# Half token tile of a dense expert layer: one float32r operand of 128 columns in place of plain float32 on column halves

## Chip, cores and metric

The kernel runs on one core of a Trainium2 chip. The metric is device time in microseconds, the median of several executions of the whole program. A profile is one execution more.

## What is computed

Two layers of a diffusion backbone over 512 latent tokens and 256 context tokens of width 1024. Each layer has a token mixer and then PEER, a retrieval over 16384 single-neuron experts. The change lies in PEER:

```python
def peer(h, wq, keys, u_tab, v_tab):
    ...
    eid = jnp.take_along_axis(cid, top_p, axis=-1)
    gate = jax.nn.softmax(top_s, axis=-1).astype(xb.dtype)
    act = jax.nn.gelu(jnp.einsum('td,thkd->thk', xb, u_tab[eid]))
    return jnp.einsum('thk,thkd->td', gate * act, v_tab[eid])
```

Every token picks 16 of the experts for each of 8 heads, 128 in all. The result is a float32 sum over them.

## The kernel before

PEER treats part of the tokens densely and part by gathers. For the dense part the scores of all 16384 experts are computed, multiplied by a weight that is zero where an expert wasn't picked, and the product with the whole table V is formed on PE (TensorE). For the gathered part rows of the tables are fetched one expert slot at a time by indirect transfers from POOL (line 1123). In layer 0 384 tokens are dense, in layer 1 320: two full tiles of 128 tokens and a half tile of 64. The other 64 slots' worth of that tile and the last tile of 128 are gathered: 192 steps over the rows of U (`gtile_u`, line 1134 on DVE) and 192 over V (`gtile_v`, line 1147 on DVE).

The dense part is `peer_x`. The experts stand in 128 blocks of 128. `ublock(i)` loads 512 KB of U (transposed) into a buffer `uv`, splits it into a float32r part `uvh` (a copy on ACT, line 113) and a residue `uvl` (a subtraction on DVE, line 114), multiplies both with the split tokens (line 121, three passes: hi x lo, lo x hi, hi x hi) and writes the GeLU of the scores to slot i of a ring `PA`/`PB`. `weights(c, i)` multiplies the weights of 8 tokens and some 44 blocks into the ring; it takes small DVE operations, eight or so on ACT, and short float16 matmuls `pwt` (line 1267). `vblock(i)` loads 512 KB of V into `uv`, splits it in the same way, splits the slot's 256 columns of the two full tiles into `wh` and `wl`, and adds twelve float32r matmuls of 512 columns to the accumulators `dacc` in PSUM, two tiles by two halves of the row by three passes. The half tile is done apart (line 1290): two plain float32 matmuls whose operands are the 64 columns of the slot and the raw block, one for each half of the row; they write to partitions 0 to 63 and 64 to 127 of one bank.

There are two buffers of `uvh`, `uvl`, `wh` and `wl`, and in layer 1 three of `uv`. A loop over m runs from -nB to 127: first weights that are due, then `vblock(m)`, then `ublock(m + R)` with R = nA + nB, the slots of the ring (32 + 46 in layer 1). So after a fill of u blocks come 50 steps with a v and a u block, some 35 v blocks with weights, and the rest of the v blocks alone. At the end the accumulators are multiplied by a gain (lines 1332 and 1335), added to the residual and normalized (`ended`, lines 1172 to 1181).

A scheduler sets the order of the instructions on every engine when the program is built, by priorities (`prio`): the dense part of layer 1 has 5, its gathers 6, so a gather step is put where the scheduler sees room. Each engine then runs its list in order. Loads of `uv` are issued by SP, each as soon as its buffer is free and those ahead of it are issued.

Of the kernel before, what the change touches and what calls it, by code (L numbers as in the profile page):

```python
# [9 lines left out]
F32 = mybir.dt.float32  # L10
F32R = mybir.dt.float32r
# [4 lines left out]
ALU = mybir.AluOpType  # L16
# [4 lines left out]
D = 1024  # L21
# [24 lines left out]
ALL, LO, HI = slice(0, 128), slice(0, 64), slice(64, 128)  # L46
# [25 lines left out]
class Kern:  # L72
# [101 lines left out]
    def schedule(self):  # L174
        a = self.a
        with ExitStack() as er:
            ec = ExitStack()
            self.context(ec, 0)
            with self.banks("ctx0", "right", w=2, S=1) as ps, ExitStack() as e0:
                md = e0.enter_context(self.pool("mod", side="right"))  # L180
                pm = e0.enter_context(self.banks("mod", "right", w=1))
                fl = e0.enter_context(self.pool("flt"))
                pf = e0.enter_context(self.banks("flt", "left", w=2, S=1))
                with self.prio(1), ExitStack() as e:
                    self.filters(fl, pf, 0, LC)
                    self.modulation(md, pm, 0, 0, 2)
                    st = self.front(e, ps, ps, 0, 1, 1, side="right")
                    self.filters(fl, pf, 0, LX)
                    self.modulation(md, pm, 0, 2, 6)
                    self.back(ps, ps, 0, 1, st, None)  # L190
                    self.filters(fl, pf, 1, LX)
                    self.modulation(md, pm, 1, 0, 2)
            self.gp = er.enter_context(self.pool("gath", side="right"))
            with self.prio(1), self.banks("rc", "right", w=2) as ps:
                gc = self.route(ps, 0, 1, "GG", side="right")
            with self.banks("x0", "left", w=2, S=2) as ps:
                with ExitStack() as e:
                    with self.prio(3):
                        pr = e.enter_context(self.banks("x0b", "right", w=2))
                        st = self.front(e, ps, pr, 0, 0, 3, split=False)  # L200
                        ex, keep = ExitStack(), ExitStack()
                        rn = self.back(ps, pr, 0, 0, st, ex, keep=keep)
                        ex = (keep, ex)
                ec.close()
            with self.prio(6):
                self.gtile_u(0, gc[0])
                self.gtile_v(0, 1, 0, gc[0])
                self.gtile_u(0, gc[1])
            with self.prio(3):
                gx, ex = self.peer_x(0, 384, 6, 31, 33, (36, 46, 46), ex, rn)  # L210
            with self.prio(6):
                self.gtile_u(0, gx[3])
                self.gtile_v(0, 0, 3, gx[3])
                self.gtile_v(0, 1, 1, gc[1])
            with ExitStack() as ec, ExitStack() as e:
                self.context(ec, 1)
                ps = e.enter_context(self.banks("x1", "left", w=2, S=2))
                pr = e.enter_context(self.banks("x1b", "right", w=2))
                with self.prio(3):
                    st = self.front(e, ps, pr, 1, 0, 4, ctx=True)  # L220
                with self.prio(4):
                    self.back(ps, pr, 1, 0, st, None, (2, 6))
            with self.prio(5):
                gx, _ = self.peer_x(1, 320, 0, 32, 46, (44, 42, 42), (ex,))
            with self.prio(6):
                for i in sorted(gx, reverse=True):
                    self.gtile_u(1, gx[i])
                    self.gtile_v(1, 0, i, gx[i])
# [955 lines left out]
    def peer_x(self, l, T, vn, nA, nB, widths, done, rn=None):  # L1184
# [4 lines left out]
        nc, a = self.nc, self.a  # L1189
        nd, half = divmod(T, 128)  # L1190
        nt = nd + bool(half)
# [4 lines left out]
        with ExitStack() as es:  # L1196
# [7 lines left out]
            free = P[0].rearrange("p i t -> p (i t)")  # L1204

            def slot(i):
                i %= nA + nB
                return P[0][:, i, :] if i < nA else P[1][:, i - nA, :]
# [62 lines left out]
                                                   1.0 / GSCALE, dst, op0=ALU.mult, op1=ALU.mult)  # L1271

            def vblock(i, sp):
                r0 = l * NEXP + i * 128
                if vn and i % vn == vn - 1:
                    raw = dn.tile([128, D], F32, name="uv", bufs=2 + l)
                    nc.sync.dma_start(raw, a["peer_v"][r0:r0 + 128, :])
                    v, w = [raw], [slot(i)]
                else:
                    raw, v = block("v", a["peer_v"][r0:r0 + 128, :])  # L1280
                    w = [sp.tile([128, nd * 128], F32R, name=n, bufs=2) for n in ("wh", "wl")]
                    self.split(*w, slot(i)[:, :nd * 128])
                vh = [[x[:, h * 512:(h + 1) * 512] for x in v] for h in range(2)]
                for t in range(nd):
                    for h in range(2):
                        self.mm([acc[t][:, h * 512:(h + 1) * 512]], [[x[:, t * 128:(t + 1) * 128] for x in w]],
                                [vh[h]], i == 0, i == 127)
                if half:
                    for h in range(2):
                        nc.tensor.matmul(acc[nd][h * 64:(h + 1) * 64], slot(i)[:, nd * 128:T],  # L1290
                                         raw[:, h * 512:(h + 1) * 512], start=(i == 0), stop=(i == 127))

            fill = (ublock(i) for i in range(nA))
            with self.banks(f"r{l}", "right", w=2, S=2) as ps:
# [5 lines left out]
            sp = ew.enter_context(self.pool(f"dw{l}"))  # L1300
            if nB:
                P.append(sp.tile([128, nB, T], F32, name="PB"))
            pa = es.enter_context(self.banks(f"da{l}", "left", w=nt - nd, S=nd))
            acc = [pa.S(f"dacc{i}") if i < nd else pa.w(f"dacc{i}") for i in range(nt)]
            due = {}
            for c, w in enumerate(widths):
                m0, m1 = cuts[c + 1] - R, cuts[c]
# [10 lines left out]
            ex = None  # L1318
            if l == 0:
                ex = ExitStack()  # L1320
                self.res[0] = ex.enter_context(self.pool("xs1", side="right")).tile([128, 4, D], F32, name="xs")
            g2, fg, *rest = (free[:, i * D:(i + 1) * D] for i in range(2 + 2 * nt))
            nc.sync.dma_start(g2, bcast_rows(self.rows[l, 3, 0, :]))
            if l:
                nc.sync.dma_start(fg, bcast_rows(a["final_g"]))
# [3 lines left out]
            for t in range(nt):  # L1329
                res, y = rest[t], rest[nt + t]  # L1330
                if t < nd:
                    nc.vector.tensor_mul(y, acc[t], g2)
                else:
                    for h in range(2):
                        nc.vector.tensor_mul(y[LO, h * 512:(h + 1) * 512], acc[t][h * 64:(h + 1) * 64],
                                             g2[h * 64:(h + 1) * 64, h * 512:(h + 1) * 512])
                self.ended(dn, l, 0, t, ALL if t < nd else LO, y, res, res if l else self.res[0][:, t, :], fg)
        return gx, ex

# [126 lines left out]
```

## Time and profile before

| | us |
|---|---|
| median of 3 runs | 4270.21 (4254.28 to 4272.61) |
| the profiled execution | 4259.61 |
| its span on the core | 4257.7 |
| PE busy | 3709.5 (87%) |
| DVE (VectorE) busy | 3508.1 (82%) |
| ACT (ScalarE) busy | 1902.7 (45%) |
| POOL busy | 1524.0 (36%) |

PE is TensorE, PEld its loads of weights, SPq the queue on which SP issues transfers. Every time is counted from the start of the span. [...]

### The profile page before, as it was taken

Reading aid. Unit: us, or ns where it says so; the run is one execution under the profiler, and the core shown is the slowest. Engines: PE = TensorE matmul, PEld = TensorE weight load, DVE = VectorE, ACT = ScalarE, POOL = GpSimd, SP = SyncE. Lnnn points to the kernel's source line nnn. Section 1 sums busy time; section 2 is a strip of 40 time slices with the busy share of each in tenths; the row PEclk is TensorE's granted clock in tenths of the full one; section 3 lists DMA queues with packets and bytes.
Section 4 is the critical chain, followed back from the end, with each engine's and each line's share of the span. In section 5 each row is a group of like instructions: output and inputs, shape, how many; then the busy total and the mean of one; then the engine's idle time right before and its main releaser. Section 6 shows DMA issues by size and latency. Waiting matters only on the chain.

```text
span 4257.7 us, 63783 instructions
## 1 busy us (share of the span) xinstructions
PE 3709.5 (87%) x22514; PEld 2804.8 (66%) x22514; DVE 3508.1 (82%) x7449; ACT 1902.7 (45%) x3719; POOL 1524.0 (36%) x1225
## 2 busy tenths in 40 slices
PE   6887988967989999988968979888888999999997
PEld 3645544557878878877756656447888877776654
DVE  5746988889899989988898875754898988898988
ACT  4555243523247426622552244633334755555732
POOL 0000345642344564366436620000126345553243
PEclk7998998979989999999989989998999999999999
DMA  6655687885768897799879952242359888888697
GB/s 204 203 178 183 214 307 244 300 288 185 250 226 266 307 363 268 243 361 348 292 233 332 348 181 87 84 142 100 138 180 352 270 296 296 294 299 277 227 352 274
DMA packets 305634, 1063.74 MB, mean 250 GB/s; under 512 B 35756, under 2 KB 42624, under 8 KB 305314
## 3 DMA queue, kind: packets, MB, share of 16 engines
q0 software_dynamic: 165888, 604.05, 40.8%
q1 hardware_dynamic: 139426, 455.61, 30.7%
q8 instruction: 177, 2.90, 0.3%
q14 instruction: 143, 1.17, 0.1%
HBM read 1042.69 MB, written 16.84 MB: 249 GB/s over the span
## 4 chain that ended last, share of the span: by engine, by line
PE 32%; DMA 21%; DVE 19%; issue 16%; POOL 6%; ACT 5%; SPq 0%; POOLq 0%; DVEq 0%; ACTq 0%
PE pst L121 7%; POOL grow L1123 6%; PE dacc L121 6%; DMA grow<-in_peer_u_dram,eid 6%; DMA grow<-in_peer_v_dram,eid 5%; DMA uv<-in_peer_v_dram 4%; PE pwin L121 4%; DMA uv<-in_peer_ut_dram 3%; DVE uvl L114 3%; DVE acc L1147 3%; DVE acc L1134 2%; PE ppq L121 2%; DMA wmod<-in_w_mod_dram 2%; PE pwo L121 1%; PE fp L414 1%
## 5 line engine op out<-in xcount | busy, mean ns | idle before, releaser
L1123 POOL DMA_INDIRECT grow<-in_peer_u_dram,eid x576 | 749.6, 1301 | 1166.6 <-DVE acc L1134 591.8
L1123 POOL DMA_INDIRECT grow<-in_peer_v_dram,eid x576 | 766.8, 1331 | 748.0 <-DVE acc L1147 604.4
L121 PE MATMUL pst<-dhT,uvh 128*128 128x384 f32 (+1 forms) x4096 | 998.6, 328 | 0.0
L113 ACT CAST uvh<-uv 128x1024 fp32r<-128x1024 f32 x491 | 512.9, 1045 | 699.7 <-DMA uv<-in_peer_v_dram 422.4
L121 PE MATMUL pst<-dhT,uvl 128*128 128x384 f32 (+1 forms) x2048 | 695.2, 339 | 115.5 <-DVE uvl L114 83.9
L1147 DVE SCALAR_TENSOR_TENSOR acc<-grow,gate,acc 128x1024 f32<-128x1024 f32 x571 | 732.9, 1283 | 49.9 <-DMA grow<-in_peer_v_dram,eid 42.9
L1134 DVE SCALAR_TENSOR_TENSOR acc<-grow,ghx 128x1024 f32<-128x1024 f32 x576 | 704.4, 1223 | 73.4 <-DMA grow<-in_peer_u_dram,eid 68.4
L121 PEld LDWEIGHTS pst<-dhT,uvh 128*128 128x128 f32 x4096 | 730.6, 192 | 2.8 <-issue 1.2
L114 DVE TENSOR_TENSOR uvl<-uv,uvh 128x1024 fp32r<-128x1024 f32 x491 | 599.5, 1222 | 154.8 <-ACT uvh L113 152.1
L121 PEld LDWEIGHTS pst<-dhT,uvl 128*128 128x128 f32 x2048 | 394.2, 192 | 218.2 <-DVE uvl L114 163.5
L121 PE MATMUL dacc<-uvh,wl 128*128 128x512 f32 x1154 | 482.0, 418 | 40.1 <-ACT uvh L113 21.3
L121 PE MATMUL dacc<-uvl,wh 128*128 128x512 f32 x1154 | 468.8, 406 | 25.7 <-DVE uvl L114 25.4
L121 PE MATMUL dacc<-uvh,wh 128*128 128x512 f32 x1154 | 462.9, 401 | 0.0
L1263 ACT ACTIVATE o<-iota,di2n 128x128 f16<-128x128 f16 x1056 | 325.2, 389 | 27.6 <-PE pwt L1267 27.4
L121 PEld LDWEIGHTS dacc<-uvh,wl 128*128 128x128 f32 x1154 | 220.6, 191 | 130.3 <-ACT uvh L113 37.0
L121 PEld LDWEIGHTS dacc<-uvl,wh 128*128 128x128 f32 x1154 | 221.1, 192 | 84.5 <-DVE uvl L114 40.2
L121 PEld LDWEIGHTS dacc<-uvh,wh 128*128 128x128 f32 x1154 | 221.2, 192 | 47.9
L1267 PEld LDWEIGHTS <-o 128*128 128x128 f16 x4224 | 126.4, 97 | 104.3 <-issue 31.1
L1233 ACT ACTIVATE PA<-pst 128x320 f32<-128x320 f32 (+1 forms) x126 | 58.4, 463 | 290.4 <-PE pst L121 290.3
L1267 PE MATMUL pwt<-og,o 128*128 128x46 f16 (+3 forms) x4224 | 152.3, 183 | 37.1 <-DVE og L1253 29.7
L1233 ACT ACTIVATE PB<-pst 128x384 f32<-128x384 f32 (+1 forms) x130 | 60.0, 462 | 218.2 <-PE pst L121 218.1
L256 POOL MEMSET rmod<- 128x512 f32 (+1 forms) x8 | 3.3, 416 | 421.1 <-PE ptmod L282 171.8
(403 smaller groups left out, 6104.5 us busy)
## 6 DMA issues: line engine op xcount, KB each, us to landing
uv<-in_peer_ut_dram SPq DMA_DIRECT2D x256, 512.0 KB
uv<-in_peer_v_dram SPq DMA_DIRECT2D x256, 512.0 KB
wmod<-in_w_mod_dram SPq DMA_DIRECT2D x96, 512.0 KB
wpq<-in_peer_wq_dram SPq DMA_DIRECT2D x48, 512.0 KB
w_in<-in_w_in_dram SPq DMA_DIRECT2D x72, 256.0 KB
w_in<-in_w_in_dram SPq DMA_DIRECT2D x18, 512.0 KB
grow<-in_peer_u_dram,eid POOLq DMA_INDIRECT x576, 6.6
grow<-in_peer_v_dram,eid POOLq DMA_INDIRECT x576, 6.8
```

The lines of the kernel that those rows point to most:

```text
L113: self.nc.scalar.copy(hi, src)
L114: self.nc.vector.tensor_tensor(lo, src, hi.bitcast(F32), op=ALU.subtract)
L121: self.nc.tensor.matmul(p, w[i], x[j], start=start and n == 0, stop=stop and n == len(passes) - 1)
L256: nc.gpsimd.memset(r, 0.0)
L414: self.nc.tensor.matmul(p, w, x, start=(i == 0), stop=(i == len(pairs) - 1))
L1123: self.nc.gpsimd.indirect_dma_start(out=r, out_offset=None, in_=self.a[table], in_offset=bass.IndirectOffsetOnAxis(ap=eid[:, j:j + 1], axi ...
L1134: nc.vector.scalar_tensor_tensor(junk, r, 1.0, hx, op0=ALU.mult, op1=ALU.mult, accum_out=dot[:, j:j + 1])
L1147: nc.vector.scalar_tensor_tensor(acc, r, w[:, j:j + 1], acc, op0=ALU.mult, op1=ALU.add)
L1233: nc.scalar.activation(slot(i), p, AF.Gelu_apprx_tanh)
L1263: nc.scalar.activation(o2[:, q], self.iota, AF.Abs, bias=i2n[:, t, k * NC + q:k * NC + q + 1])
L1267: nc.tensor.matmul(p[:, q, :], o2[:, q, :], og[:, g, q, :], start=(g == 0), stop=(g == 1))
```

## The change

In layer 1 the copy on ACT now takes all 320 columns of the slot into one tile `both`, and DVE writes the residue of the half tile's 64 columns right behind their copies and the residue of the 256 columns at the end. The 128 columns in the middle (64 copies, 64 residues) are one operand. It is multiplied with `uvl` and with `uvh` for each half of the row: four float32r matmuls, into a third accumulator of two banks that holds the sums of the copies on partitions 0 to 63 and those of the residues on 64 to 127. At the end both are multiplied by the gain and added. `nB` of layer 1 goes from 46 to 45. Layer 0, without a half tile, gets the tile `both` too, with the same copy and the same single subtraction.

```diff
--- before.py
+++ after.py
@@ -221,7 +221,7 @@
                 with self.prio(4):
                     self.back(ps, pr, 1, 0, st, None, (2, 6))
             with self.prio(5):
-                gx, _ = self.peer_x(1, 320, 0, 32, 46, (44, 42, 42), (ex,))
+                gx, _ = self.peer_x(1, 320, 0, 32, 45, (44, 42, 42), (ex,))
             with self.prio(6):
                 for i in sorted(gx, reverse=True):
                     self.gtile_u(1, gx[i])
@@ -1271,15 +1271,23 @@
                                                    1.0 / GSCALE, dst, op0=ALU.mult, op1=ALU.mult)
 
             def vblock(i, sp):
                 r0 = l * NEXP + i * 128
+                F = nd * 128
                 if vn and i % vn == vn - 1:
                     raw = dn.tile([128, D], F32, name="uv", bufs=2 + l)
                     nc.sync.dma_start(raw, a["peer_v"][r0:r0 + 128, :])
                     v, w = [raw], [slot(i)]
                 else:
                     raw, v = block("v", a["peer_v"][r0:r0 + 128, :])
-                    w = [sp.tile([128, nd * 128], F32R, name=n, bufs=2) for n in ("wh", "wl")]
-                    self.split(*w, slot(i)[:, :nd * 128])
+                    both = sp.tile([128, 2 * T], F32R, name="w", bufs=2)
+                    w = [both[:, :F], both[:, 2 * T - F:]]
+                    nc.scalar.copy(both[:, :T], slot(i))
+                    for o, n, to in ((F, T - F, T), (0, F, 2 * T - F)):
+                        if n:
+                            nc.vector.tensor_tensor(both[:, to:to + n], slot(i)[:, o:o + n],
+                                                    both[:, o:o + n].bitcast(F32), op=ALU.subtract)
                 vh = [[x[:, h * 512:(h + 1) * 512] for x in v] for h in range(2)]
                 for t in range(nd):
                     for h in range(2):
@@ -1287,8 +1295,9 @@
                                 [vh[h]], i == 0, i == 127)
                 if half:
                     for h in range(2):
-                        nc.tensor.matmul(acc[nd][h * 64:(h + 1) * 64], slot(i)[:, nd * 128:T],
-                                         raw[:, h * 512:(h + 1) * 512], start=(i == 0), stop=(i == 127))
+                        for k in (1, 0):
+                            nc.tensor.matmul(acc[nd][:, h * 512:(h + 1) * 512], both[:, F:F + 128], vh[h][k],
+                                             start=(i == 0 and k == 1), stop=(i == 127 and k == 0))
 
             fill = (ublock(i) for i in range(nA))
             with self.banks(f"r{l}", "right", w=2, S=2) as ps:
@@ -1300,8 +1309,8 @@
             sp = ew.enter_context(self.pool(f"dw{l}"))
             if nB:
                 P.append(sp.tile([128, nB, T], F32, name="PB"))
-            pa = es.enter_context(self.banks(f"da{l}", "left", w=nt - nd, S=nd))
-            acc = [pa.S(f"dacc{i}") if i < nd else pa.w(f"dacc{i}") for i in range(nt)]
+            pa = es.enter_context(self.banks(f"da{l}", "left", w=0, S=nt))
+            acc = [pa.S(f"dacc{i}") for i in range(nt)]
             due = {}
             for c, w in enumerate(widths):
                 m0, m1 = cuts[c + 1] - R, cuts[c]
@@ -1319,7 +1328,7 @@
             if l == 0:
                 ex = ExitStack()
                 self.res[0] = ex.enter_context(self.pool("xs1", side="right")).tile([128, 4, D], F32, name="xs")
-            g2, fg, *rest = (free[:, i * D:(i + 1) * D] for i in range(2 + 2 * nt))
+            g2, fg, *rest = (free[:, i * D:(i + 1) * D] for i in range(3 + 2 * nt))
             nc.sync.dma_start(g2, bcast_rows(self.rows[l, 3, 0, :]))
             if l:
                 nc.sync.dma_start(fg, bcast_rows(a["final_g"]))
@@ -1331,9 +1340,10 @@
                 if t < nd:
                     nc.vector.tensor_mul(y, acc[t], g2)
                 else:
-                    for h in range(2):
-                        nc.vector.tensor_mul(y[LO, h * 512:(h + 1) * 512], acc[t][h * 64:(h + 1) * 64],
-                                             g2[h * 64:(h + 1) * 64, h * 512:(h + 1) * 512])
+                    more = rest[2 * nt]
+                    nc.vector.tensor_mul(y[LO], acc[t][LO], g2[LO])
+                    nc.vector.tensor_mul(more[LO], acc[t][HI], g2[HI])
+                    nc.vector.tensor_add(y[LO], y[LO], more[LO])
                 self.ended(dn, l, 0, t, ALL if t < nd else LO, y, res, res if l else self.res[0][:, t, :], fg)
         return gx, ex
```

The order on DVE in the last v blocks of layer 1 (`uvl` is the residue of a V block, `wl` or `w` that of the weights, line 1147 a gather step). Before:

```order
L114 TENSOR_TENSOR wl<-PB,wh 128x256
L1147 SCALAR_TENSOR_TENSOR acc<-grow,gate,acc 128x1024
L114 TENSOR_TENSOR uvl<-uv,uvh 128x1024
L1147 SCALAR_TENSOR_TENSOR acc<-grow,gate,acc 128x1024
L114 TENSOR_TENSOR wl<-PB,wh 128x256
```

With the change:

```order
L114 TENSOR_TENSOR uvl<-uv,uvh 128x1024
L1289 TENSOR_TENSOR w<-PB,w 128x64
L1289 TENSOR_TENSOR w<-PB,w 128x256
L1147 SCALAR_TENSOR_TENSOR acc<-grow,gate,acc 128x1024 x2
L114 TENSOR_TENSOR uvl<-uv,uvh 128x1024
```

The weights' residue moved from ahead of its block's `uvl` to behind it, and became two rows; over the last 40 blocks there are 1.83 gather steps a block before and 1.7 with the change.

The end of DVE's list, from its last residues on. Before:

```order
L114 TENSOR_TENSOR uvl<-uv,uvh 128x1024
L1147 SCALAR_TENSOR_TENSOR acc<-grow,gate,acc 128x1024 x2
L1332 TENSOR_TENSOR PA<-dacc_28941,PA 128x1024
...
L1335 TENSOR_TENSOR PA<-dacc_28943,PA 64x512
L105 TENSOR_SCALAR nrm<-nss 128x1
L1147 SCALAR_TENSOR_TENSOR acc<-grow,gate,acc 128x1024
L1172 TENSOR_TENSOR PA<-PA 64x1024
L106 RECIPROCAL nry<-nry 128x1 x2
L1147 SCALAR_TENSOR_TENSOR acc<-grow,gate,acc 128x1024
...
L1154 COPY grow<-acc 64x1024
```

With the change:

```order
L1289 TENSOR_TENSOR w<-PB,w 128x256
L1147 SCALAR_TENSOR_TENSOR acc<-grow,gate,acc 128x1024 x2
L1341 TENSOR_TENSOR PA<-dacc_28834,PA 128x1024
...
L1345 TENSOR_TENSOR PA<-dacc_28836,PA 64x1024
L1147 SCALAR_TENSOR_TENSOR acc<-grow,gate,acc 128x1024
...
L108 SCALAR_TENSOR_TENSOR nry<-nrt,nry 64x1
L1180 SCALAR_TENSOR_TENSOR PA<-PA,nry 64x1024
L1147 SCALAR_TENSOR_TENSOR acc<-grow,gate,acc 128x1024 x11
L1154 COPY grow<-acc 64x1024
L1155 TENSOR_TENSOR acc<-acc,grow 64x1024
```

Of the gather steps, 4 stood behind the last `uvl` before, and 18 do with the change.

SP's list in the joint loop of layer 1, with what each load waits for (DMAHW is a count of earlier transfers). Before:

```order
L1224 DMA uv<-in_peer_v_dram 128x1024 [waits DMAHW2_49,PE_49]
L1224 DMA uv<-in_peer_ut_dram 128x1024 [waits DMAHW5_49,DVE_49]
L1224 DMA uv<-in_peer_v_dram 128x1024 [waits DMAHW4_49,PE_49]
L1224 DMA uv<-in_peer_ut_dram 128x1024 [waits DMAHW7_49,DVE_49]
L1224 DMA uv<-in_peer_v_dram 128x1024 [waits DMAHW6_49,PE_49]
```

With the change:

```order
L1224 DMA uv<-in_peer_ut_dram 128x1024 [waits DMAHW5_49,DVE_49]
L1224 DMA uv<-in_peer_v_dram 128x1024 [waits DMAHW6_49,DVE_49]
L1224 DMA uv<-in_peer_ut_dram 128x1024 [waits DMAHW7_49,DVE_49]
L1224 DMA uv<-in_peer_v_dram 128x1024 [waits DMAHW0_49,DVE_49]
L1224 DMA uv<-in_peer_ut_dram 128x1024 [waits DMAHW1_49,DVE_49]
```

The loads keep their order and wait for DVE alone.

## Rows read from the trace of the kernel before

**Rows 1.** Windows by stage: fill, A, B, C; length, then busy (instructions), PEclk, DMA share, GB/s.

```profile
core 0: us, PE busy (x) PEld busy (x) DVE busy (x) ACT busy (x) POOL busy (x), PEclk, DMA share, GB/s
3300.00:3450.00 150.00, 138.08 (x1369) 131.24 (x1370) 144.87 (x292) 107.68 (x238) 47.70 (x43) 1.00 0.80 267
...
3539.10:3792.00 252.90, 242.06 (x1729) 189.97 (x1728) 227.77 (x321) 140.65 (x273) 130.74 (x81) 1.00 0.85 292
3937.40:4025.40 88.00, 88.00 (x673) 56.23 (x672) 81.23 (x175) 66.31 (x144) 19.99 (x17) 1.00 0.68 221
4070.10:4200.70 130.60, 122.96 (x481) 71.31 (x480) 111.23 (x123) 42.52 (x61) 59.84 (x54) 1.00 0.94 341
```

**Rows 2.** Windows of line 1290 alone in A, B, C: PE busy (records), PEld busy.

```profile
3539.10:3792.00 252.90, 32.37 (x120) 5.93 (x120) 1.00 0.85 292
3937.40:4025.40 88.00, 21.58 (x80) 3.96 (x80) 1.00 0.68 221
4070.10:4200.70 130.60, 32.37 (x120) 5.93 (x120) 1.00 0.94 341
```

**Rows 3.** Timeline of PE in C: start, duration, engine, line, operation, output and inputs.

```profile
4101.33 0.39 PE L121 MATMUL dacc<-uvl,wh 128*128 128x512 f32 x1
4101.56 0.40 PE L121 MATMUL dacc<-uvh,wh 128*128 128x512 f32 x1
4101.88 1.08 PE L1290 MATMUL dacc<-uv,PA 128*64 128x512 f32 x4
4102.89 0.49 PE L121 MATMUL dacc<-uvh,wl 128*128 128x512 f32 x1
4103.23 0.40 PE L121 MATMUL dacc<-uvl,wh 128*128 128x512 f32 x1
...
4105.85 1.08 PE L1290 MATMUL dacc<-uv,PA 128*64 128x512 f32 x4
```

**Rows 4.** Waits of SP, 4040 to 4232 us (C): us in total, times, longest.

```profile
SPq L1224 <- PE dacc L1290: 151.2, 41, 3.9
```

**Rows 5.** Timeline of DVE, SP, ACT and PE in A, 3639 to 3651 us.

```profile
3639.79 1.23 DVE L114 TENSOR_TENSOR uvl<-uv,uvh 128x1024 fp32r<-128x1024 f32 x1
3641.04 0.33 SPq L1224 DMA_DIRECT2D uv<-in_peer_ut_dram  x1
3647.98 1.05 ACT L113 CAST uvh<-uv 128x1024 fp32r<-128x1024 f32 x1 [2.41 <-DMA uv<-in_peer_ut_dram]
3649.06 1.23 DVE L114 TENSOR_TENSOR uvl<-uv,uvh 128x1024 fp32r<-128x1024 f32 x1 [2.31 <-ACT uvh L113]
3650.31 0.33 SPq L1224 DMA_DIRECT2D uv<-in_peer_ut_dram  x1
3650.34 0.41 PE L121 MATMUL pst<-dhT,uvl 128*128 128x320 f32 x1 [0.97 <-DVE uvl L114]
```

**Rows 6.** Timeline of PE in B.

```profile
3923.62 0.40 PE L121 MATMUL dacc<-uvh,wh 128*128 128x512 f32 x1
3923.94 1.08 PE L1290 MATMUL dacc<-uv,PB 128*64 128x512 f32 x4
3924.95 0.57 PE L1267 MATMUL pwt<-og,o 128*128 128x42 f16 x16
```

**Rows 7.** Timeline of DVE in A.

```profile
3642.19 1.22 DVE L114 TENSOR_TENSOR uvl<-uv,uvh 128x1024 fp32r<-128x1024 f32 x1
3643.32 0.42 DVE L114 TENSOR_TENSOR wl<-PA,wh 128x256 fp32r<-128x256 f32 x1
3643.66 2.60 DVE L1147 SCALAR_TENSOR_TENSOR acc<-grow,gate,acc 128x1024 f32<-128x1024 f32 x2
```

**Rows 8.** Windows of line 1123 (gathers) in layer 0: POOL busy (gathers), PEclk, DMA share, GB/s.

```profile
800.00:850.00 50.00, 33.57 (x28) 1.00 0.90 320
1500.00:1550.00 50.00, 32.56 (x26) 1.00 0.98 368
```

**Rows 9.** Timeline of DVE in the tail; the span ends at 4257.7.

```profile
4231.48 2.35 DVE L1332 TENSOR_TENSOR PA<-dacc,PA 128x1024 f32<-128x1024 f32 x2
4236.01 0.68 DVE L1335 TENSOR_TENSOR PA<-dacc,PA 64x512 f32<-64x512 f32 x1
4252.57 1.29 DVE L1180 SCALAR_TENSOR_TENSOR grow<-grow,nry 64x1024 f32<-64x1024 f32 x1
```

## Prediction

> **What bounds the kernel now.** I read the page's 40 slices first, to see which engine is full where, then the busy time by stretch, then the timeline of single blocks. Only layer 1 has a half token tile (T = 320), so the change can act only behind about 3300 us. That part has four stages. The fill makes scores (u blocks alone). Stage A, 50 steps, holds one u block and one v block each; stage B is about 35 v blocks with weights beside them; stage C is the last 43 v blocks. Then comes the tail. Gather steps of the other 192 token slots (two DVE instructions per slot, lines 1134 and 1147) run on DVE between all of this.
>
> In the fill DVE is busy 144.87 of 150 us, 96.6%: that is how full this DVE gets when it is the bound [rows 1]. In the three later stretches it has 90, 92 and 85%. Every v block issues four records of line 1290, so 120, 80 and 120 of them are 30, 20 and 30 blocks [rows 2], and the step is 252.9/30 = 8.43 us in A, 88/20 = 4.40 in B, 130.6/30 = 4.35 in C.
>
> What holds each stage differs. B is PE's: busy in all 88 us [rows 1]. In C a block without a wait takes 4105.85 - 4101.88 = 3.97 us [rows 3], yet the mean is 4.35: loads are late. A load of the next block may start only when its buffer is free, and SP waits 151.2 us in C for line 1290, the half tile's plain float32 matmuls, which read the raw block and stand last in it [rows 4]. In A it is the u load. The u load goes out at 3641.04, at the end of the residue of the u block before it (3639.79 + 1.23); its copy on ACT starts at 3647.98, its residue at 3649.06, PE starts on it at 3650.34 after an idle 0.97 us, and the next u load goes out at 3650.31 [rows 5]. That is a ring of 9.27 us with a single buffer in it, though three exist. The waits in the built order say why: u loads wait for DVE alone, v loads for PE. The addresses of the tiles confirm it: through most of A all u blocks take one of the three buffers and the v blocks alternate over the other two.
>
> **The change part by part.** *PE.* In C the distance from the last float32r matmul before the pair to the second one after it is 4103.23 - 4101.56 = 1.67 us, where two ordinary slots are 2 x 0.23 [rows 3], so the pair with its changes of mode costs 1.21 us. Four float32r matmuls of 512 columns at 0.23 are 0.92: 0.29 us less per block. In B the next thing is a float16 matmul: 3924.95 - 3923.62 = 1.33, less one slot 0.23, is 1.10 [rows 6], so 0.18 less. A is between the two.
>
> *DVE.* The residue of the weights becomes two subtractions, 64 and 256 columns. From start to start 1024 columns take 3643.32 - 3642.19 = 1.13 us and 256 take 0.34 [rows 7], so 1.03 ns a column, and 64 take 0.34 - 0.20 = 0.14 us: 18 us for 128 blocks. The bounds are 0.07 (columns alone) and 0.34 (no cheaper than 256), 8 and 44 us; I take 0.14, for the two rows give the fixed part. [...]
>
> *The order on DVE.* The scheduler answered. Behind the last residue of layer 1 stood 4 gather steps; now 18 stand there. So 14 steps of 1.28 us [rows 7], 18 us, leave the dense stages just as 18 us of new subtractions enter: DVE's work there stays what it was, and the tail gets the 14 steps.
>
> *Loads.* The half tile's matmuls now read the split parts, so a raw block is free after its residue and no load waits for PE. In the built addresses the buffers now rotate over all three in A and C. In A that breaks the ring of one buffer. What is late next is DVE.
>
> *ACT.* Its copy has 320 columns for 256: at 1.05 us for 1024 [rows 5] some 0.07 us more, on an engine that is busy 56% in A and 33% in C [rows 1]; hidden, and 9 us if it were not. SP moves nothing by itself, POOL keeps its order, one score block goes from the fill into A (nB 45), where it costs the same: 0. The three accumulators now fill the PSUM that is left, before the first v block needs them: 0. Layer 0 has no half tile, its order is the same: 0.
>
> **The sum**, by stage. *A*: DVE has 227.77/30 = 7.59 us of work a step [rows 1], plus 0.14, at 96.6% is 8.0; PE has 242.06/30 = 8.07, less 0.2 to 0.3, is 7.8. I take 8.0, so 0.43 x 50 = 21 us less (bounds: 8.4, nothing, and 7.8, 31). *B*: PE 4.40 - 0.18 = 4.22, DVE (81.23/20 + 0.14)/0.966 = 4.35; 2 us less (0 to 6). *C*: PE 3.97 - 0.29 = 3.68. DVE 111.23/30 = 3.71, plus 0.14, less 0.13 gather steps a block (1.7 in the new order for 1.83), is 3.69, at 96.6% 3.8. Transfers: 341 GB/s x 4.35 us is 1.48 MB a block, 1.42 without the 0.13 step; the best sustained rate of the trace is 368 GB/s [rows 8], so 3.85. I take 3.9: 0.45 x 43 = 19 us less (10 to 26). *Tail*: the old one runs from 4231.48 to the end of the span, 26 us [rows 9]. Thirteen more steps in it at 1.2 to 1.28 are 16; the half tile's last multiplies become two multiplies and an addition of 1024 columns on 64 partitions, 3.4 us for two of 0.68 [rows 9], plus 2; a final scaling of 1.3 moves forward, less 1. If gathers come only at the pace where little else loads, 28 in 50 us [rows 8], 1.79 each, it is up to 6 more. I take 19 us more (16 to 23). Together 42 - 19 = 23 us less than the profiled execution's 4259.6: 4237. That execution stands 10.6 us below the median of the three runs, 4270.2, so for a median I say **4247 us**.
>
> **The rivals.** *Everything follows PE and the loads.* DVE's idle share shrinks to 2%: A 7.8, B 4.25, C 3.75, so 31 + 5 + 26 - 19 = 43 us less: 4227. For it: DVE's waits in A are mostly waits for that u load. Against: two full engines rarely interleave that well, and C would need 1.42/3.75 = 379 GB/s.
>
> *The pair was already as cheap.* PE gains nothing, and only the freed loads help: A 8.15 and C 4.1, 14 + 11 - 19 = 6 us less: 4264. For it: the four records of the pair begin and end within 1.08 us, near the 0.92 of four passes [rows 3]; only the gaps around them, 0.1 each side, speak for the change. [...]
>
> *Slower: DVE's queue holds the dense stages.* DVE works in order. Before, the weights' residue of a block stood ahead of that block's own residue, with a gather step between; now both subtractions of the weights stand right behind it, and PE's first matmul waits for the last of them. From PE's release of the parts to the next use but one: copy 1.05, residue 1.13, 0.14 and 0.34, some 2.8 us with the semaphores, and 4.0 where a gather step of 1.25 is in front. That decides once it is more than PE's 3.68 in most blocks. Then the stages keep their lengths, and the tail's 19 to 23 us are lost: 4289 to 4293. Against it: in C DVE is idle 15% of the time now.
>
> **How the numbers follow.** The forecast has 0.42 (its own range 4235 to 4260), everything on PE 0.15, the pair already cheap 0.27, slower 0.16. Half a per cent, about what a measurement can tell here, is 21 us: below 4249 lie somewhat over half of the forecast and all of the first rival, 0.42 with a little of the second; above 4291.6 lies some half of the last, 0.09; the rest, 0.49, is the same. The range 4216 to 4286 reaches below the first rival and into the last one, and leaves out under 0.2.
>
> **What would show it.** In the profile after: line 1299 in place of line 1290 with four matmuls a block 0.23 us apart and no gap around them; the step of A near 8.0 with PE's wait for the u residue gone; C's step near 3.9 at over 355 GB/s, and no wait of SP for PE there; 15 gather steps behind the accumulators' last multiplies and some 45 us from these to the end. I am wrong if A's step stays over 8.3 (DVE, not the u load, held it), if C stays over 4.1, or if the tail is under 35 us.

## The result and the profile after

The changed kernel takes **4217.57 us** (median of 4 runs, 4214.54 to 4221.55) against 4271.41 us for the kernel before on the same chip (4254.28 to 4280.67): a ratio of 0.9878, 95% interval 0.9853 to 0.9903. It is faster by 1.2%, 54 us, where 23 were forecast (4247 against a median before of 4270.2). In a later session it was run again: ratio 0.9888 (0.9868 to 0.9908).

The page's busy times and its last row of bandwidth, after:

```profile
PE 3659.5 (87%) x22514; PEld 2875.9 (68%) x22514; DVE 3525.9 (84%) x7578; ACT 1900.8 (45%) x3719; POOL 1535.0 (36%) x1225
...
GB/s 206 206 181 187 218 308 256 293 283 193 241 213 277 304 356 285 234 357 348 311 214 330 338 233 94 68 146 99 83 244 242 315 276 357 314 308 308 228 378 270
```

DVE has 18 us more work than before, in a span that is 45 us shorter, and the last slice but one moves 378 GB/s. The windows of the fill, A, B, C and the tail (length, busy time and instructions of each engine, PEclk, DMA share, GB/s), to be set beside [rows 1]; the three in the middle are 30, 20 and 30 blocks again:

```profile
core 0: us, PE busy (x) PEld busy (x) DVE busy (x) ACT busy (x) POOL busy (x), PEclk, DMA share, GB/s
3300.00:3450.00 150.00, 138.52 (x1411) 131.44 (x1410) 144.81 (x292) 110.64 (x245) 48.19 (x43) 1.00 0.81 271
3532.20:3765.20 233.00, 233.00 (x1746) 209.17 (x1745) 229.54 (x353) 139.68 (x275) 113.22 (x79) 1.00 0.88 311
3893.90:3978.70 84.80, 84.80 (x689) 67.67 (x688) 82.81 (x195) 65.96 (x145) 13.21 (x14) 1.00 0.70 217
4018.00:4132.40 114.40, 111.94 (x482) 88.86 (x480) 109.52 (x158) 42.45 (x61) 72.49 (x51) 1.00 1.00 378
4160.00:4212.00 52.00, 0.00 (x0) 0.00 (x0) 39.03 (x47) 6.92 (x13) 17.72 (x12) 0.52 0.57 188
```

And those of line 1299, whose four matmuls a block stand in the place of line 1290's four records [rows 2]:

```profile
3532.20:3765.20 233.00, 32.51 (x121) 22.55 (x121) 1.00 0.88 311
3893.90:3978.70 84.80, 21.63 (x80) 15.03 (x80) 1.00 0.70 217
4018.00:4132.40 114.40, 33.47 (x121) 21.91 (x120) 1.00 1.00 378
```

The steps are 233/30 = 7.77 us in A (before 8.43), 84.8/20 = 4.24 in B (4.40) and 114.4/30 = 3.81 in C (4.35). In A PE is busy in all 233 us, and DVE in 98.5% of them. In C the DMA engines are full, at 378 GB/s.

SP's waits from 4000 to 4160 us (C), in place of [rows 4], have no line of PE left; but for 0.4 us the loads wait for DVE alone, as the change would have it:

```profile
SPq L1224 <- DVE uvl L114: 82.4, 26, 4.4
SPq L1224 <- DVE w L1289: 47.5, 12, 4.4
```

To see where the time went I cut layer 1 at four instructions that every kernel here has: the first matmul of the half tile behind the other passes of V's blocks 0, 50, 85 and 127 (the first block of A, B, C and the last of C; where TensorE had them all done ahead of those passes, one just ahead). A cut is good to about 1 us. This also takes out what happens ahead of them: between profiled runs of different kernels, block 0 starts anywhere from 3457 to 3479 us, though nothing ahead of layer 1 differs. Lengths in us:

| kernel | A, blocks 0 to 50 | B, 50 to 85 | C, 85 to 127 | tail, to the end | sum |
|---|---|---|---|---|---|
| before | 425.4 | 162.1 | 184.7 | 25.8 | 797.9 |
| after | 390.3 | 152.6 | 159.6 | 53.5 | 755.9 |
| difference | -35.1 | -9.5 | -25.1 | +27.7 | -42.0 |

Block 0 itself starts 3 us earlier (3459.8 against 3456.8), which lies within that spread and is no gain of the change. The experiments below are cut in the same way; their lines are collected in a table behind them.

### The profile page after: what moved, and what is told of

It is laid out like the page before. It is cut to its first block, busy times and chain, and to the rows that moved or that the text cites. A ratio compares the mean times of both kernels' runs of the same rounds, so it can differ in the third digit from the quotient of the medians.

```text
span 4212.7 us, 64061 instructions
## 1 busy us (share of the span) xinstructions
PE 3659.5 (87%) x22514; PEld 2875.9 (68%) x22514; DVE 3525.9 (84%) x7578; ACT 1900.8 (45%) x3719; POOL 1535.0 (36%) x1225
## 4 chain that ended last, share of the span: by engine, by line
PE 35%; DVE 18%; issue 18%; DMA 17%; POOL 8%; ACT 4%; SPq 0%; POOLq 0%; DVEq 0%; ACTq 0%
PE pst L121 9%; POOL grow L1123 8%; PE dacc L121 8%; DMA grow<-in_peer_u_dram,eid 7%; DMA grow<-in_peer_v_dram,eid 6%; PE pwin L121 4%; DVE acc L1134 2%; PE ppq L121 2%; DVE acc L1147 2%; DVE uvl L114 2%; PE pwt L1267 2%; PE pwo L121 1%; PE dacc L1299 1%; DMA uv<-in_peer_v_dram 1%; PE fp L414 1%
## 5 line engine op out<-in xcount | busy, mean ns | idle before, releaser
L121 PE MATMUL dacc<-uvh,w 128*128 128x512 f32 x2308 | 789.3, 408 | 39.6 <-DVE w L1289 24.2
L121 PEld LDWEIGHTS dacc<-uvh,w 128*128 128x128 f32 x2308 | 441.3, 192 | 146.7 <-DVE w L1289 28.5
L121 PEld LDWEIGHTS pst<-dhT,uvl 128*128 128x128 f32 x2048 | 394.0, 192 | 164.2 <-DVE uvl L114 124.5
L121 PE MATMUL dacc<-uvl,w 128*128 128x512 f32 x1154 | 467.2, 405 | 18.0 <-DVE uvl L114 17.8
L121 PEld LDWEIGHTS dacc<-uvl,w 128*128 128x128 f32 x1154 | 221.3, 192 | 72.7 <-DVE uvl L114 27.1
L1267 PEld LDWEIGHTS <-o 128*128 128x128 f16 x4224 | 126.4, 97 | 88.0 <-issue 27.9
L121 PE MATMUL pwin<-hT,w_inh 128*128 128x256 f32 (+1 forms) x576 | 148.9, 349 | 0.7 <-DVE hT L114 0.7
L113 ACT CAST wpqh<-wpq 128x256 fp32r<-128x256 f32 x192 | 75.4, 405 | 149.3 <-PE ppq L121 97.9
```

The source lines that it names most:

```text
L113: self.nc.scalar.copy(hi, src)
L121: self.nc.tensor.matmul(p, w[i], x[j], start=start and n == 0, stop=stop and n == len(passes) - 1)
L1267: nc.tensor.matmul(p[:, q, :], o2[:, q, :], og[:, g, q, :], start=(g == 0), stop=(g == 1))
```

## The experiments

Two theories. **Buffers**: the raw blocks that come free early, and so turn over all three buffers, give the gain. **Pair**: TensorE's cheaper half tile gives it.

**e1, the raw block freed, the pair as it was.**

```diff
-                                         raw[:, h * 512:(h + 1) * 512], start=(i == 0), stop=(i == 127))
+                                         vh[h][0].bitcast(F32), start=(i == 0), stop=(i == 127))
```

> The kernel before, but the half tile's pair of matmuls (line 1290) reads the float32r high part of V's block in place of the raw block: the pair stays two plain matmuls on column halves, with its instructions as they were, and the raw block is free as soon as its split is done, so that all three raw buffers pass between U and V as in the change. Left out: the low part of V in the half tile's result. Theory 'buffers' (most of the dense gain comes from raw blocks that come free early, the cheaper pair only lowers a floor): the step of the joint loop falls from 8.43 us to 8.0 to 8.1 (what TensorE needs for it with the old pair), that of the last V blocks from 4.35 to 4.0, so 50 x 0.38 + 43 x 0.35 = 34 us less, about 4237 us, and SyncE's waits of loads of V on the pair are gone. Theory 'pair' (the gain is TensorE's 0.2 to 0.29 us a block, 128 times): nothing of it is here, steps of 8.4 and 4.35 us, 4265 to 4275 us. If the plain pair on float32r data were itself cheaper, its spacing in the trace would show it.

Measured: 4226.50 us, ratio 0.9891 (0.9860 to 0.9922). That is nearly all of the change's gain, without its cheaper pair, and more than the 34 us that the theory of the buffers gave it: A and C bring 18 and 17, and B and the tail 8 and 6 besides. The same three stretches of its windows:

```profile
3546.00:3780.00 234.00, 234.00 (x1687) 184.39 (x1687) 222.37 (x313) 132.98 (x261) 107.39 (x80) 1.00 0.89 310
3892.00:3980.00 88.00, 88.00 (x674) 56.17 (x672) 82.15 (x174) 63.86 (x141) 16.30 (x17) 1.00 0.69 222
4037.00:4160.00 123.00, 122.42 (x493) 73.12 (x494) 113.52 (x128) 45.39 (x63) 76.81 (x57) 1.00 1.00 379
```

PE is now busy all the time in A and nearly so in C; 41 of the 42 steps of C are between 3.96 and 3.98 us, which [rows 3] showed as a block without a wait. So the old pair keeps its price (B's step is 4.36 us as before), and what went are the waits. SP's, from 4037 to 4200 us, are on DVE:

```profile
SPq L1224 <- DVE uvl L114: 114.9, 34, 4.0
SPq L1224 <- DVE wl L114: 11.6, 2, 6.0
```

**e2, the buffers in turn, the raw block held as before.**

```diff
...
-                raw = dn.tile([128, D], F32, name="uv", bufs=2 + l)
+                if l:
+                    turn[0] += 1
+                    raw = dn.tile([128, D], F32, name=f"uv{turn[0] % 3}")
+                else:
+                    raw = dn.tile([128, D], F32, name="uv", bufs=2)
```

> The kernel before, but the raw blocks of the last layer take the three buffers in turn by a counter, in place of U on one and V on two; the pair still reads the raw block and so holds it until TensorE is past it. Theory 'buffers, by the turn': the joint loop's single buffer for U is what its 8.43 us hang on: 8.1 to 8.2 us there, 12 to 17 us less in all (4255 to 4259 us), the last V blocks unchanged at 4.35. Theory 'buffers, by the hold': the raw block that TensorE holds is what delays the loads, so nothing moves: 8.4 us and 4.35 us, 4265 to 4275 us. Theory 'pair': nothing moves either.

Measured: 4299.62 us, ratio 1.0055 (1.0038 to 1.0073), slower. No theory had that. A is longest of all here, 449 us. SP's loads, the copies and residues of U's blocks and the pair in two steps of it:

```profile
3600.48 0.33 SPq L1230 DMA_DIRECT2D uv<-in_peer_v_dram  x1
3600.90 0.38 SPq L1230 DMA_DIRECT2D uv<-in_peer_ut_dram  x1
3607.38 1.04 ACT L113 CAST uvh<-uv 128x1024 fp32r<-128x1024 f32 x1 [2.61 <-DMA uv<-in_peer_ut_dram]
3607.48 1.08 PE L1296 MATMUL dacc<-uv,PA 128*64 128x512 f32 x4
3608.45 1.22 DVE L114 TENSOR_TENSOR uvl<-uv,uvh 128x1024 fp32r<-128x1024 f32 x1 [1.98 <-ACT uvh L113]
3609.70 0.33 SPq L1230 DMA_DIRECT2D uv<-in_peer_v_dram  x1
3610.12 0.38 SPq L1230 DMA_DIRECT2D uv<-in_peer_ut_dram  x1
3616.48 1.99 ACT L113 CAST uvh<-uv 128x1024 fp32r<-128x1024 f32 x2 [2.49 <-DMA uv<-in_peer_ut_dram]
```

U's load now goes out right behind V's, and its copy starts 6.48 us later, about as late as in the old ring [rows 5]. V's load in turn goes out at the end of the residue of the U block before it (3608.45 + 1.22 = 3609.67), and the pair had ended by then (3607.48 + 1.08 = 3608.56). So in these steps the turn has put V's load behind U's residue and U's next load behind V's: a ring with one load of U in it stays. In A (3546 to 3780 us) SP waits for TensorE for little:

```profile
SPq L1230 <- PE dacc L1296: 8.7, 3, 7.2
```

Why the built order of the loads came out so isn't shown.

**e3, the change with U back on one buffer in the joint loop.** The tile is named by a counter; `n` counts the blocks, `u` and `v` bound the joint loop.

```diff
...
+                    k = n % 3 if n < u or n >= u + 2 * v else 1 if name == "u" else n // 2 % 2 * 2
+                    raw = dn.tile([128, D], F32, name=f"uv{k}")
...
```

> The change, but in the joint loop of the last layer the raw blocks of U keep one buffer and those of V the two others, as in the kernel before; everything else of the change is kept, the cheaper pair too, and V's raw block is free after its split. Theory 'buffers, by the turn': U's next load waits for U's split in the one buffer, a joint step of 8.2 us or more, so 50 x 0.45 = 22 us above the change, about 4240 us. Theory 'pair' (or 'buffers, by the hold' alone): the joint step stays at 7.8 us, 4215 to 4220 us.

Measured: 4255.03 us, ratio 0.9962 (0.9942 to 0.9981). A is 421.9 us, nearly the 425.4 of before, though it has the cheap pair; B (152.5), C (160.1) and the tail (50.8) are those of the change. In A (3546 to 3780 us) ACT's wait for U's load is back, of which the change has none; of the second line the change has 2.1 us:

```profile
ACT uvh L113 <- DMA uv<-in_peer_ut_dram: 23.8, 21, 2.4
DVE uvl L114 <- ACT uvh L113: 14.0, 16, 2.1
```

So in A the turn of three is worth 32 us, on top of the early release and of the cheap pair; the sum of the stages is 29 us above the change's, where 22 were expected.

**e4, a control: the change's other number alone.**

```diff
-                gx, _ = self.peer_x(1, 320, 0, 32, 46, (44, 42, 42), (ex,))
+                gx, _ = self.peer_x(1, 320, 0, 32, 45, (44, 42, 42), (ex,))
```

> The kernel before with the change's other number alone (45 in place of 46 kept activations of the joint loop). Both theories: within 0.3% of the kernel before, steps of 8.4 and 4.35 us; one block moves from one stage to the next. If this alone gained 10 us or more, the stage lengths and not the pair would be the cause.

Measured: 4275.44 us, ratio 1.0002 (0.9984 to 1.0020). It does nothing to the time.

**e5 and e9, the change with the hold given back, and its control.** Behind the four passes of a block, except the first and the last, stands one small plain matmul with zeros. In e5 (first edit) it reads the raw block, in e9 (second) the high part:

```diff
...
+                        if 0 < i < 127:
+                            nc.tensor.matmul(acc[nd][:32, :32], zero[0], raw[:, :32], start=False, stop=False)
```
```diff
...
+                            nc.tensor.matmul(acc[nd][:32, :32], zero[0], vh[0][0].bitcast(F32)[:, :32], start=False, stop=False)
```

> The change, plus one small plain matmul behind the half tile's four: 32 columns of zeros against 32 columns of V's raw block, added to the half tile's sum (it adds nothing, but it holds the raw block until TensorE is past it, as the old pair did; so U is back on one buffer in the joint loop and V on two). Theory 'buffers': the gain of the loads is lost although the four cheap passes stay: a joint step of 8.3 us or more with SyncE waiting on TensorE for V's loads, 4.2 us or more in the last V blocks; 4245 to 4270 us. Theory 'pair': the step rises by the small matmul's own time alone, which the spacing of the records shows (0.1 to 0.4 us by the neighbourhood of the old pair, 1.21 us for two of 512 columns), and TensorE stays without waits: 4220 to 4250 us. The step and TensorE's waits in the joint loop decide, not the time alone.

> The kernel with the small plain matmul of 32 columns, but reading V's high part (which TensorE's passes hold anyway) in place of the raw block: TensorE's added time is the same as there (0.37 us a block: joint steps of 8.07 us against 7.70), and nothing holds the raw block. Theory 'buffers': most of what that kernel lost comes back, the last V blocks fall from 4.43 us to 4.1 or less, 4235 to 4255 us. Theory 'pair' (the added TensorE time is what cost): the same time as with the raw block, 4290 to 4305 us.

Measured: with the hold 4302.41 us, ratio 1.0054 (1.0028 to 1.0080); without it 4243.34 us, ratio 0.9942 (0.9924 to 0.9961). TensorE does the same work in both. They ran on different chips, so their ratios to the kernel before are compared: the hold alone costs 1.0054 - 0.9942 = 1.1%, 48 us, and 822.6 - 774.5 = 48 us in the sum of the stages. That is nearly all that the change gains. With the hold the time is above the range of either theory. SP's waits from 4050 to 4200 us, with the hold:

```profile
SPq L1224 <- PE dacc L1308: 113.6, 29, 6.3
```

and without it:

```profile
SPq L1224 <- DVE uvl L114: 107.9, 30, 4.4
```

C is 201.0 us against 171.8, steps of 4.79 and 4.09. One number of the theory missed: in A most steps are 8.07 us in both, not 8.3 or more. There the small matmul alone lifts TensorE's need from 7.69 to 8.07, and the hold adds 14 us over the stage (416.6 against 402.9).

**e6, half of the half tile's passes.**

```diff
-                        for k in (1, 0):
-                            nc.tensor.matmul(acc[nd][:, h * 512:(h + 1) * 512], both[:, F:F + 128], vh[h][k],
-                                             start=(i == 0 and k == 1), stop=(i == 127 and k == 0))
+                        nc.tensor.matmul(acc[nd][:, h * 512:(h + 1) * 512], both[:, F:F + 128], vh[h][0],
+                                         start=(i == 0), stop=(i == 127))
```

> The change with two of the half tile's four passes (the low part of V's block is left out of the half tile's result): TensorE's need falls by 2 x 0.23 = 0.46 us a block, with no instruction of another engine touched, though the scheduler may place the gather steps anew. If TensorE is the bound of the changed kernel's dense stages: joint step 7.7 to 7.25, next stage 4.2 to 3.75, and some 35 to 40 us less (4180 us). If VectorE is (98% busy in the joint loop): the steps move by less than 0.1 us or what they give comes back as gather steps in the tail, 4205 to 4225 us.

Measured: 4237.34 us, ratio 0.9905 (0.9876 to 0.9934), no faster than the change. Both halves of the expectation came true at once. TensorE does bound A and B: the steps fall to 7.23 and 3.72 us, by just the two passes. But the gain comes back whole: the passes of the last block start at 4109 us, and 56 gather steps stand behind it in DVE's order, where the change has 18. Its windows of A, C and the tail:

```profile
3546.00:3770.00 224.00, 224.00 (x1715) 202.34 (x1713) 220.55 (x350) 141.05 (x275) 107.74 (x70) 1.00 0.89 308
4000.00:4108.00 108.00, 106.57 (x446) 81.84 (x446) 107.11 (x184) 46.64 (x66) 69.54 (x48) 1.00 1.00 386
4110.00:4224.70 114.70, 2.49 (x11) 1.69 (x9) 90.69 (x88) 6.92 (x13) 66.14 (x51) 0.53 0.77 267
```

DVE is at 98.5% in A and 99% in C while TensorE works, and then runs on alone for 115 us.

**e7 and e11 (one kernel, two sessions), the 64 columns on GpSimd; e10, the change beside e11; e8, both subtractions of the last layer on GpSimd.**

```diff
-                            nc.vector.tensor_tensor(both[:, to:to + n], slot(i)[:, o:o + n],
+                            (nc.gpsimd if n == 64 else nc.vector).tensor_tensor(both[:, to:to + n], slot(i)[:, o:o + n],
```
```diff
-                            nc.vector.tensor_tensor(both[:, to:to + n], slot(i)[:, o:o + n],
+                            (nc.gpsimd if l else nc.vector).tensor_tensor(both[:, to:to + n], slot(i)[:, o:o + n],
```

> The change with the 64-column subtraction of both layers' V blocks on GpSimd in place of VectorE: VectorE has 0.13 us less in each of 248 blocks, 128 of them in the last layer. If VectorE is the bound: 10 to 17 us less in the last layer, 4200 to 4208 us. If TensorE or the loads are: 4213 to 4222 us. GpSimd's own price for it shows in no run yet; if it came late, TensorE would wait for the weights and the time would rise.

> The change with the 64-column subtractions on GpSimd again, beside the change. If VectorE's 0.13 us a block count, 8 to 15 us under the change; if the DMA engines set the last V blocks (they are full there in both, at 378 GB/s) and only the joint loop gains, within 5 us of it.

> The change itself again, beside the next kernel on one chip. 4210 to 4222 us by either theory.

> The change with both subtractions of the last layer's V weights on GpSimd: VectorE has 0.47 us less in each of 128 blocks, 60 us of work. If VectorE is the bound: 30 to 50 us less (4170 to 4190 us), with a shorter tail, since the gather steps fit beside the dense work. If TensorE or the loads are: 4210 to 4222 us. If GpSimd is slow at it and the gathers that it issues queue behind it: above 4230 us.

Layer 0 has no half tile and so none of the 64-column subtractions: e7 and e11 touch the last layer's 128 blocks alone, not 248.

Measured: the 64 columns on GpSimd 4214.25 us, ratio 0.9847 (0.9817 to 0.9877), then 4200.35, ratio 0.9833 (0.9807 to 0.9859), with the change at 4221.27, ratio 0.9888 (0.9868 to 0.9908), on the same chip. The second pair of intervals does not overlap: this version beats both kernels, by 21 us over the change, where 8 to 15 were expected of DVE's share; e7 alone, at 4214, hadn't decided it. Beside the change's profile of that session, A and C are 4 us longer each (394.0 and 165.0 against 389.8 and 161.1), and the tail is 29.1 us against 53.0: 5 gather steps stand in it, not 18. With both subtractions there it is 4266.86 us, ratio 0.9977 (0.9960 to 0.9994). GpSimd's groups between 4050 and 4150 us in that kernel, with the mean ns of one behind the busy time:

```profile
L1289 POOL TENSOR_TENSOR w<-PA,w 128x256 fp32r<-128x256 f32 x20 | 27.0, 1350 | 0.0
L1289 POOL TENSOR_TENSOR w<-PA,w 128x64 fp32r<-128x64 f32 x20 | 9.4, 472 | 0.3
```

and waits of TensorE and DVE from 4050 to 4200 us:

```profile
PEld dacc L121 <- POOL w L1289: 31.7, 25, 3.0
DVE acc L1147 <- DMA grow<-in_peer_v_dram,eid: 21.5, 22, 2.4
PE dacc L121 <- POOL w L1289: 21.2, 22, 2.5
```

GpSimd needs 1.35 us where DVE's next start came 0.34 us later [rows 7]; TensorE waits for the weights, and DVE for gathers.

All of them by stage, with the gather steps that stand behind the last residue of layer 1 in DVE's order:

| kernel | A | B | C | tail | sum | gather steps in the tail |
|---|---|---|---|---|---|---|
| before | 425.4 | 162.1 | 184.7 | 25.8 | 797.9 | 4 |
| after | 390.3 | 152.6 | 159.6 | 53.5 | 755.9 | 18 |
| e1, freed, old pair | 407.4 | 153.8 | 167.5 | 19.7 | 748.4 | 1 |
| e2, turn with hold | 449.3 | 163.1 | 183.1 | 27.9 | 823.4 | 6 |
| e3, U on one buffer | 421.9 | 152.5 | 160.1 | 50.8 | 785.2 | 18 |
| e4, nB 45 alone | 431.6 | 158.6 | 184.2 | 27.8 | 802.2 | 6 |
| e5, change with hold | 416.6 | 163.6 | 201.0 | 41.4 | 822.6 | 11 |
| e9, control of e5 | 402.9 | 161.4 | 171.8 | 38.4 | 774.5 | 10 |
| e6, two passes | 363.5 | 143.2 | 135.4 | 115.7 | 757.8 | 56 |
| e7, 64 columns on GpSimd | 395.0 | 154.0 | 165.2 | 29.0 | 743.3 | 5 |
| e8, both subtractions there | 409.8 | 173.5 | 193.2 | 17.4 | 793.9 | 0 |
| e10, the change again | 389.8 | 152.4 | 161.1 | 53.0 | 756.3 | 18 |
| e11, e7's kernel again | 394.0 | 152.5 | 165.0 | 29.1 | 740.6 | 5 |

Each row is one execution. The change and e10 are the same kernel and lie 1.5 us apart or less, e7 and e11 up to 3; e4, whose time is that of the kernel before, has 6 us more in A and 4 more in the sum. So single differences of a few us are no result.

## Why the prediction was right and wrong

**The direction and the mechanism were right; the size was less than half.** Against the profiled execution the sum was -23 us, and it came to -45: A -35 for -21, B -9.5 for -2, C -25 for -19, the tail +27.7 for +19, and 3 us ahead of block 0, which are no gain of the change. Then 10.6 us were added for a median; the profiled execution after stands only 3.0 below its own. That is the spread between executions and nothing of the mechanism. Together these make the 29 us between 4247 and 4218.

**The step that failed** is "DVE is busy 144.87 of 150 us, 96.6%: that is how full this DVE gets when it is the bound". It set A at 8.0 and B at 4.35. After the change DVE is busy 229.54/233 = 98.5% in A and 82.81/84.8 = 97.7% in B, and it bounds neither: PE is busy in all of both, and e6 moved both steps by just what it took from PE. 96.6% is the fill's own share (96.5% after), and no ceiling. The better numbers stood in the same paragraph: PE's "7.8" for A and "4.22" for B; 7.77 and 4.24 were measured. The first rival, **everything follows PE and the loads** (7.8, 4.25, 3.75; measured 7.77, 4.24, 3.81), was the right one: 31 + 5 + 26 - 19 = 43 us, against 35 + 9.5 + 25 + 3 - 27.7 = 45 measured. That its total fits to 2 us is luck in part: its stages were 7.5 us short, the tail took 8.7 more than it had, and the 3 ahead of block 0 are chance. What spoke against it, "two full engines rarely interleave that well", was my estimate; in A PE was at 100% and DVE at 98.5%.

**The pair's price was right.** The passes in C stand 0.23 us apart from start to start (the records, of 0.39, overlap), without the gap ahead of the pair in [rows 3]; the 0.34 behind the last one is no rule, most in C are 0.23 too:

```profile
4061.97 0.39 PE L121 MATMUL dacc<-uvh,w 128*128 128x512 f32 x1
4062.20 0.39 PE L1299 MATMUL dacc<-uvl,w 128*128 128x512 f32 x1
...
4062.89 0.40 PE L1299 MATMUL dacc<-uvh,w 128*128 128x512 f32 x1
4063.23 0.47 PE L121 MATMUL dacc<-uvh,w 128*128 128x512 f32 x1
```

From e1 to the change, B's steps go from 4.36 to 4.18 and A's from 7.98 to 7.69: the 0.18 and 0.29 us of the working. So the rival "the pair was already as cheap" falls. The two halves of the pair do overlap: their first records begin 0.01 us apart, at 4101.88 and 4101.89 us, and last 0.64 us each. Even so the pair took 1.01 us up to the start of the next pass, and 0.2 more in the gaps on both sides [rows 3], against 0.92 for the four passes. What makes the gaps, "changes of mode" in the prediction, no run shows.

**The new subtraction was right.** DVE in C, after:

```profile
4057.27 1.22 DVE L114 TENSOR_TENSOR uvl<-uv,uvh 128x1024 fp32r<-128x1024 f32 x1
4058.41 0.55 DVE L1289 TENSOR_TENSOR w<-PA,w 128x64 fp32r<-128x64 f32 x2
4058.88 2.60 DVE L1147 SCALAR_TENSOR_TENSOR acc<-grow,gate,acc 128x1024 f32<-128x1024 f32 x2
```

Both parts together take 4058.88 - 4058.41 = 0.47 us, so the 64 columns 0.13 beside the 0.34 of 256: 0.14 was taken. A record of the 64 columns lasts 0.22 us (at 4139.89 us), which is more than its pace, since records overlap: it and the next one, of 0.42, span 0.55.

**The loads were right, and are the larger part.** U's ring in A and TensorE's hold in C are what the change removes: e1 does that alone and has the change's time within the intervals, and e5 gives the hold back and loses 48 us. In A neither cause stands alone: the old pair with free turning buffers gives 425.4 - 407.4 = 18 us (e1), the cheap pair with U on one buffer 425.4 - 421.9 = 3.5 (e3), which is not clear of the spread between executions, and both 35. The rival **slower: DVE's queue holds the dense stages** falls with that; PE's largest wait for the weights' residue in C (4000 to 4160 us) is small:

```profile
PEld dacc L1299 <- DVE w L1289: 4.8, 12, 1.2
```

**C** came to 3.81 for 3.9. The cap "the best sustained rate of the trace is 368 GB/s" was too low: 378 with the DMA engines full, and 386 in e6. It was also misread: the trace before has a faster stretch of the same length, ahead of the fill.

```profile
3245.00:3295.00 50.00, 44.92 (x293) 42.96 (x294) 44.18 (x64) 17.60 (x26) 38.02 (x25) 1.00 1.02 396
```

**The tail** was undersized: "thirteen more steps in it at 1.2 to 1.28". With little beside them DVE waits for the gathers: 14 more steps came with 27.7 us; less the 1 us net that the other edits were given, that is 1.9 each, and from e1 to e6 it is (115.7 - 19.7)/55 = 1.75. That is the pace of [rows 8], 1.79, which I had kept for the upper end. In the change's tail (from 4158 us) DVE waits 8.0 us for gathers, and in that of the kernel before (from 4231 us) not at all; with 14 steps of 1.28, 17.9 us, that is 25.9 of the 27.7. The waits, and two lines of the tail:

```profile
DVE acc L1147 <- DMA grow<-in_peer_v_dram,eid: 8.0, 6, 4.6
...
4191.92 1.28 DVE L1147 SCALAR_TENSOR_TENSOR acc<-grow,gate,acc 128x1024 f32<-128x1024 f32 x1 [0.35 <-DMA grow<-in_peer_v_dram,eid]
4197.86 1.29 DVE L1147 SCALAR_TENSOR_TENSOR acc<-grow,gate,acc 128x1024 f32<-128x1024 f32 x1 [4.65 <-DMA grow<-in_peer_v_dram,eid]
```

**Where the cheap pair's gain went.** Beside e1 the change has 17 us less in A, 1 in B and 8 in C, and 34 more in the tail: it is given back. The dense stages end earlier, but the gather steps that ran beside them are DVE's and the transfers' work and remain to be done. e6 shows it once more at a larger size, and e11 from the other side: 128 x 0.13 = 17 us taken from DVE, 15.7 us less in the sum (756.3 - 740.6). So a part of the 34 us is the price of the new subtraction. Without it on DVE the cheap pair pays: the sums of e7 and e11 are 5 and 8 us under e1's, and their ratios 0.9847 and 0.9833 against 0.9891; the interval of e11 lies below that of e1, that of e7 doesn't.

**Still open**: why e2 is slower than before was read from one pair of steps and not tried further; and why one buffer for U costs 32 us in A in e3, but 14 in e5 over e9, isn't shown. That TensorE's higher need in e5 covers it is only argued; what fits is that four loads of U in a row there, from 3666.94 to 3690.90 us, go out 7.99 us apart on average, no slower than TensorE's step of 8.07.

## What to carry over

Look first at who is the last reader of a loaded block: here a late reader held the buffer, and the load behind it, and that cost 48 us (e5 over e9), more than the 26 us that the cheaper reader saved in the dense stages (e1 to the change). A share of busy time from another stage is no ceiling (96.6% in the fill, 98.5% in A); take an engine's work per step as its floor, and let the largest floor set the step (PE's 7.8 and 4.22 us, where 7.77 and 4.24 were measured). Where a second stream of work fills the gaps of a first, count what a faster first leaves for the tail: here 14 gather steps moved there, at 1.9 us each, near the gathers' own pace of 1.79 [rows 8]. Take work from the engine that both need: the 64 columns on GpSimd gave 21 us (e11 beside e10).

## What the runs showed of the hardware that I had not expected

- A plain float32 matmul of only 32 columns among float32r passes raised the joint step from 7.69 to 8.07 us (e9); its two records span 0.25 us.
- One core moved 378 GB/s for 114 us (the change) and 386 for 108 us (e6), with the DMA engines at 1.00, and 396 for 50 us in the kernel before, at 1.02.
- Two full engines interleaved in the changed kernel: in A PE at 100% and DVE at 98.5% over 233 us.
- GpSimd took 0.47 (e8) to 0.62 us (e11) for a subtraction of 64 columns and 1.35 (e8) for 256; DVE's next start came 0.13 and 0.34 us later.
